# RMSNorm over 16384 rows of 512 on one core: few large transfers, and a first store that waits for a 256-byte marker transfer

## The chip, the cores and the metric

The kernel runs on one core of a Trainium2 chip. The metric is the device time of one execution in microseconds (us); the time before is 161.68 us, the median of three runs (161.65 to 161.87). The core has a matrix engine (PE), a vector engine (VectorE, DVE in the profile), a scalar engine (ScalarE, ACT), GpSimd (POOL) and SyncE (SP). Here SP does no arithmetic: it issues all DMA transfers, in program order, and waits for semaphores before it issues them. 16 DMA engines move the data between device memory (DRAM) and the on-chip memory SBUF.

## What is computed

```python
def reference(x, gamma):                # x: 16 x 1024 x 512 float32, gamma: 512 (ones)
    eps = 1e-5
    rms = np.sqrt(np.mean(x ** 2, axis=-1, keepdims=True) + eps)
    return (x / rms * gamma).astype(np.float32)
```

Each of the 16384 rows of 512 numbers is divided by the root of its mean square and multiplied by gamma. x has 33.55 MB, and the output as much again.

## The kernel before

**Tiles.** The rows are cut into four tiles t = 0 to 3. In a tile each of the 128 partitions holds R = 32 consecutive rows, 64 KB in one piece in DRAM and in SBUF. A whole tile is 8.39 MB. SBUF has three slots of that size; tile 3 goes into slot 0 again, so its loads wait until the stores of tile 0 from the same rows have landed. Everything is done in place: x is loaded into a slot, scaled there, and stored from there.

**Transfers.** `load(t, slot, r0, r1)` (line 45) and `store(t, slot, r0, r1)` (line 49) move rows r0 to r1 of all 128 partitions. One such transfer is 128 descriptors, one for each partition, 2 KB times the number of rows each, eight on each of the 16 DMA engines. All go through SP's one queue. gamma is brought as a single row, in five pieces (line 58), each a single descriptor on one DMA engine. The list before loads row 0, rows 1 to 7, gamma, rows 8 to 15 and rows 16 to 31 of tile 0, then the first half of tile 1. Then, in `transfers`, come stores of one single row of tile 0 between the next loads. The rest of tile 0 is stored in two pieces, tile 3 is loaded in two halves, and tiles 1 and 2 are stored whole and tile 3 in halves.

**Groups.** The arithmetic goes by groups of rows, `(t, first row, rows, pieces, share)`: `pieces` says how many rows the ScalarE and VectorE instructions for the sums of squares take at a time, `share` how many rows at the end of the group GpSimd scales. For one group:

- `square_sums`: ScalarE squares a piece into a scratch tile (line 96), VectorE adds it up along the row (line 97). A piece of 7 or 4 rows goes to PSUM (the memory that the matrix engine writes), a piece of 5 to its own SBUF tile, and a piece of 9 rows into rows 23 to 31 of slot 2, which is free as long as tile 2 has not been loaded there.
- `inverse_rms`: ScalarE takes the root (line 102), VectorE the reciprocal (line 103).
- `scale_by_pool`: GpSimd multiplies its share of the rows by the reciprocal (line 109) and by gamma (line 110).
- `scale` and `times_gamma`: ScalarE multiplies the other rows one by one by the reciprocal (line 118), then VectorE multiplies them all by gamma (line 122), which a matmul of ones with the gamma row has spread over the partitions in PSUM (line 66).

The order is written by hand (`manual_schedule`). While group k is scaled, the squares of group k+1 are taken; `transfers(t, g)` of group k is called after its `times_gamma`, so its DMAs follow all earlier DMAs in SP's order. The engines run their own instructions in that order and wait for each other by semaphores. DMA transfers use eight semaphores in turn, so the ninth transfer waits until the first has landed.

Of the kernel before, what the change touches and what calls it, by code (L numbers as in the profile page):

```python
# [9 lines left out]
def kernel(  # L10
# [6 lines left out]
    nc = tc.nc  # L17
    P = nc.NUM_PARTITIONS
    eps = 1e-5
    fp32 = mybir.dt.float32  # L20
# [4 lines left out]
    of = out.flatten_outer_dims()  # L25
    N, D = xf.shape
# [9 lines left out]
    const = ctx.enter_context(tc.tile_pool(name="const", bufs=1))  # L36
# [7 lines left out]
    def load(t, slot, r0, r1):  # L44
        dma = nc.sync.dma_start(out=slots[slot][:, r0:r1], in_=xv[t][:, r0:r1])  # L45
        before_scale.append((slot, r0, r1, dma))

    def store(t, slot, r0, r1):
        dma = nc.sync.dma_start(out=ov[t][:, r0:r1], in_=slots[slot][:, r0:r1])
        before_scale.append((slot, r0, r1, dma))  # L50

    gamma_row = const.tile([1, D], fp32)
    pieces = (0, 128, 224, 320, 416, D)

    load(0, 0, 0, 1)
    load(0, 0, 1, 8)
    for c0, c1 in zip(pieces, pieces[1:]):
        nc.sync.dma_start(out=gamma_row[:, c0:c1], in_=gamma.unsqueeze(0)[:, c0:c1])
    load(0, 0, 8, 16)
    load(0, 0, 16, 32)  # L60
    load(1, 1, 0, 16)

    ones_col = const.tile([1, P], fp32)
    nc.gpsimd.memset(ones_col, 1.0)  # L64
# [9 lines left out]


    groups = [
        (0, 0, 7, (7,), 3),
        (0, 7, 9, (9,), 5),
        (0, 16, 16, (7, 9), 7),
        (1, 0, 16, (7, 9), 7),  # L80
        (1, 16, 16, (7, 5, 4), 7),
        (2, 0, 16, (7, 5, 4), 7),
        (2, 16, 16, (7, 5, 4), 7),
# [36 lines left out]
    def times_gamma(t, g, r0, r1):  # L120
# [4 lines left out]
        for slot, b0, b1, earlier in before_scale:  # L125
            if slot == slot_of[t] and b0 < g + r1 and g + r0 < b1:
                tc.declare_no_dep(scaled.ins, earlier.ins, reason="ScalarE waited for it before it scaled these rows")

    def transfers(t, g):
        if (t, g) == (0, 0):  # L130
            store(0, 0, 0, 1)
            load(1, 1, 16, 32)
            store(0, 0, 1, 2)
            load(2, 2, 0, 23)
        elif (t, g) == (0, 16):
            store(0, 0, 2, 3)
            load(2, 2, 23, 32)
            store(0, 0, 3, 16)
            store(0, 0, 16, 32)
            load(3, 0, 0, 16)  # L140
            load(3, 0, 16, 32)
        elif (t, g) == (1, 16):
            store(1, 1, 0, 32)
        elif (t, g) == (2, 16):
            store(2, 2, 0, 32)
        elif (t, g) == (3, 0):
            store(3, 0, 0, 16)
        elif (t, g) == (3, 16):
            store(3, 0, 16, 32)
# [16 lines left out]
    for k, group in enumerate(groups):  # L166
        t, g, n, pieces, share = group
        mine = n - share
        half = (mine + 1) // 2
        ahead = groups[k + 1 :][:1]  # L170
        ss, todo = pieces_of(ahead[0]) if ahead else (None, [])
        scale_by_pool(rstd, t, g, n, share)
        for piece in todo[:2]:
            square_sums(*piece)
        scale(rstd, t, g, 0, half)
        for piece in todo[2:]:
            square_sums(*piece)
        scale(rstd, t, g, half, mine)
        times_gamma(t, g, 0, mine)
        transfers(t, g)  # L180
        for nxt in ahead:
            rstd = inverse_rms(ss, nxt[2])
# [30 lines left out]
```

## Time and profile before

| what | value |
|---|---|
| runs | 161.65, 161.68, 161.87 us |
| profiled execution, first to last instruction (span; its only time on the page) | 160.2 us |
| VectorE busy | 112.0 us, 70% |
| ScalarE busy | 107.8 us, 67% |
| GpSimd busy | 106.4 us, 66% |
| PE busy | 2.0 us |
| HBM read and written | 33.56 MB and 33.55 MB |
| first DMA issue, last DMA issue (SP) | 0.74 us, 139.2 us |

The profiled execution is a separate execution; the page gives its span, from the first to the last instruction. The runs measure the whole execution, which includes what lies before and after. The DMA rows of the page say how busy the 16 DMA engines were on average. The trace also keeps each DMA packet (a descriptor's start, duration and bytes) and each increment of a transfer's semaphore, sixteen for a transfer over all engines; "landed" here means that the last of the sixteen has come. Times are in us from the start of the span.

### The profile page before, as it was taken

What the parts mean: (1) busy time and instruction counts of PE and PEld (TensorE: products, weight loads), DVE (VectorE), ACT (ScalarE), POOL (GpSimd) and SP (SyncE); (2) the same over time, 40 slices, a digit from 0 to 9 for tenths busy, and PEclk for the clock granted to TensorE, in tenths of its full rate; (3) what the DMA queues carried; (4) which work ended last, traced back from release to release, by engine and by line L of the source; (5) the groups of instructions that cost most, each with busy time, mean ns of one, the idle gap of its engine ahead of it and who ended that gap; (6) DMA issues with size and microseconds to landing.
All of it is one profiled execution on the core that took longest, in us unless ns stands there. A gap on an engine that the chain in (4) does not pass through costs nothing.

```text
span 160.2 us, 276 instructions
## 1 busy us (share of the span) xinstructions
PE 2.0 (1%) x2; PEld 0.5 (0%) x2; DVE 112.0 (70%) x39; ACT 107.8 (67%) x108; POOL 106.4 (66%) x24
## 2 busy tenths in 40 slices
PE   0050000000000000000000000000000000000000
PEld 0010000000000000000000000000000000000000
DVE  0018098899798999999999999999999009700000
ACT  3071967976999998999899899989960990000000
POOL 1000951994999599999999999999999980000000
DMA  5999999899999899999999999996996996999994
GB/s 189 431 421 475 442 401 458 340 446 491 417 435 494 388 379 383 426 450 475 434 401 426 483 401 393 524 491 295 524 491 295 524 491 295 401 491 417 401 450 196
DMA packets 2747, 67.12 MB, mean 419 GB/s; under 512 B 313, under 2 KB 314, under 8 KB 826
## 3 DMA queue, kind: packets, MB, share of 16 engines
q1 hardware_dynamic: 2746, 67.11, 98.1%
q14 instruction: 1, 0.01, 0.0%
HBM read 33.56 MB, written 33.55 MB: 419 GB/s over the span
## 4 chain that ended last, share of the span: by engine, by line
DVE 59%; ACT 22%; DMA 4%; ACTq 0%; issue 0%; SPq 0%
DVE ss L97 36%; DVE slot L122 23%; ACT slot L118 8%; ACT slot L96 7%; ACT sq_psum L96 6%; DMA slot<-in_x_dram 4%; DVE ss L103 1%; ACT ss L102 1%; ACTq L208 0%; ACT gamma_b L165 0%; SPq L45 0%; ACTq L96 0%
## 5 line engine op out<-in xcount | busy, mean ns | idle before, releaser
L109 POOL TENSOR_TENSOR slot<-slot,ss 128x3584 f32<-128x3584 f32 (+2 forms) x9 | 47.0, 5218 | 24.1 <-DVE ss L103 24.1
L110 POOL TENSOR_TENSOR slot<-slot,gamma_b 128x3584 f32<-128x3584 f32 (+2 forms) x9 | 59.3, 6587 | 0.7
L97 DVE TENSOR_REDUCE ss<-sq_psum 128x7 f32<-128x3584 f32 (+1 forms) x13 | 42.2, 3247 | 13.7 <-ACT sq_psum L96 13.7
L118 ACT ACTIVATE slot<-slot,ss 128x512 f32<-128x512 f32 x75 | 47.3, 706 | 4.7 <-DVE ss L103 4.7
L122 DVE TENSOR_TENSOR slot<-slot,gamma_psum 128x4608 f32<-128x4608 f32 (+2 forms) x9 | 41.3, 4590 | 8.7 <-ACT slot L118 8.7
L96 ACT ACTIVATE sq_psum<-slot 128x3584 f32<-128x3584 f32 (+1 forms) x13 | 34.6, 2658 | 6.4 <-DMA slot<-in_x_dram 5.7
L97 DVE TENSOR_REDUCE ss<-slot 128x9 f32<-128x4608 f32 x3 | 14.9, 4954 | 4.4 <-ACT slot L96 4.2
L97 DVE TENSOR_REDUCE ss<-sq_sbuf 128x5 f32<-128x2560 f32 x5 | 14.0, 2803 | 0.0
L96 ACT ACTIVATE slot<-slot 128x4608 f32<-128x4608 f32 x3 | 12.1, 4033 | 0.0
L96 ACT ACTIVATE sq_sbuf<-slot 128x2560 f32<-128x2560 f32 x5 | 11.6, 2321 | 0.0
L102 ACT ACTIVATE ss<-ss,eps_t 128x16 f32<-128x16 f32 (+2 forms) x9 | 2.7, 305 | 11.9 <-DVE ss L97 11.9
L103 DVE RECIPROCAL ss<-ss 128x16 f32<-128x16 f32 (+2 forms) x9 | 2.1, 236 | 0.4 <-ACT ss L102 0.4
L66 PE MATMUL gamma_psum<-gamma_row,ones_col 1*128 1x512 f32 x2 | 2.0, 1122 | 8.6 <-DMA gamma_row<-in_gamma_dram 8.6
L72 ACT ACT_TABLE_LOAD x1 | 1.3, 1283 | 1.2 <-PEq L197 1.2
L165 ACT COPY gamma_b<-gamma_psum 128x512 f32<-128x512 f32 x1 | 0.6, 567 | 0.0
L66 PEld LDWEIGHTS gamma_psum<-gamma_row,ones_col 1*128 1x128 f32 x2 | 0.5, 308 | 8.6 <-issue 8.6
L64 POOL MEMSET ones_col<- 1x128 f32 x1 | 0.2, 195 | 0.3 <-POOLq L197 0.3
L197 POOL MEMSET const-float32-0.0<- 128x1 f32 x1 | 0.1, 99 | 0.2 <-issue 0.2
L72 ACT ACTIVATE table<-eps_t 128x1 f32<-128x1 f32 x1 | 0.2, 202 | 0.0
L197 POOL MEMSET const-bfloat16-1.0<- 128x1 bf16 x1 | 0.1, 102 | 0.0
L197 POOL MEMSET const-uint8-127<- 128x1 uint8 x1 | 0.1, 102 | 0.0
L197 POOL MEMSET const-float32-1.0<- 128x1 f32 x1 | 0.1, 99 | 0.0
(1 smaller groups left out, 0.1 us busy)
## 6 DMA issues: line engine op xcount, KB each, us to landing
slot<-in_x_dram SPq DMA_DIRECT2D x5, 4096.0 KB, 21.9
out_dram<-slot SPq DMA_DIRECT2D x3, 4096.0 KB, 23.4
slot<-in_x_dram SPq DMA_DIRECT2D x1, 5888.0 KB
out_dram<-slot SPq DMA_DIRECT2D x1, 3328.0 KB, 21.8
slot<-in_x_dram SPq DMA_DIRECT2D x1, 2304.0 KB, 14.3
slot<-in_x_dram SPq DMA_DIRECT2D x1, 2048.0 KB, 9.9
slot<-in_x_dram SPq DMA_DIRECT2D x1, 1792.0 KB, 7.0
out_dram<-slot SPq DMA_DIRECT2D x3, 256.0 KB
```

The lines of the kernel that those rows point to most:

```text
L66: nc.tensor.matmul(gamma_psum[:, 0], ones_col, gamma_row, start=True, stop=True)
L72: nc.scalar.activation(out=table, in_=eps_t, func=AF.Sqrt)
L96: nc.scalar.activation(out=sq[:, :m], in_=rows, func=AF.Square)
L97: nc.vector.tensor_reduce(out=ss[:, r : r + m, 0], in_=sq[:, :m], axis=mybir.AxisListType.X, op=OP.add)
L102: nc.scalar.activation(out=ss[:, :n, 0], in_=ss[:, :n, 0], func=AF.Sqrt, bias=eps_t, scale=1.0 / D)
L103: nc.vector.reciprocal(out=ss[:, :n, 0], in_=ss[:, :n, 0])
L109: nc.gpsimd.tensor_tensor(out=part, in0=part, in1=by_row, op=OP.mult)
L110: last = nc.gpsimd.tensor_tensor(out=part, in0=part, in1=gamma_b.to_broadcast([P, share, D]), op=OP.mult)
L118: nc.scalar.activation(out=x[:, g + r, :], in_=x[:, g + r, :], func=AF.Copy, scale=rstd[:, r])
L122: scaled = nc.vector.tensor_tensor(out=part, in0=part, in1=gamma_psum.to_broadcast([P, r1 - r0, D]), op=OP.mult)
L165: nc.scalar.copy(out=gamma_b[:, 0], in_=gamma_psum[:, 0])
L197: nc = _bacc.Bacc("TRN2", target_bir_lowering=False, num_devices=1)
```

## The change

The transfers are fewer and larger, one wait is added twice, and two groups become one.

- Tile 0's first half is one load of 16 rows (before: rows 0, 1 to 7, 8 to 15), gamma one piece of 2 KB (before: five). All of tile 1 is loaded ahead of the first group; before, its second half came behind a one-row store.
- The three one-row stores of tile 0 are gone. Tile 2 is loaded as 28 and 4 rows (before 23 and 9), tile 0 stored as 27 and 5 rows (before 1, 1, 1, 13 and 16), tile 3 loaded as 27 and 5 rows (before 16 and 16).
- Between the two loads of tile 2 stands a load of 64 numbers of gamma (256 bytes) into a small tile `mark` that nothing reads. The store of tile 0's rows 0 to 26 waits for it.
- The store of tile 1 waits for the load of tile 3's first 27 rows.
- The first two groups (7 rows and 9 rows, GpSimd shares 3 and 5) become one of 16 rows with a share of 7. The group of tile 1's first half takes its squares in pieces of 7, 5, 4 instead of 7, 9.

```diff
@@ load, store, first loads
-    def store(t, slot, r0, r1):
+    def store(t, slot, r0, r1, behind=None):
         dma = nc.sync.dma_start(out=ov[t][:, r0:r1], in_=slots[slot][:, r0:r1])
         before_scale.append((slot, r0, r1, dma))
+        if behind is not None:
+            tc.add_manual_dep(
+                dma.ins,
+                behind.ins.name,
+                mybir.DependencyInfo(mybir.DependencyClass.Sync, mybir.DependencyReason.DATA),
...
+            )
-    pieces = (0, 128, 224, 320, 416, D)
-    load(0, 0, 0, 1)
-    load(0, 0, 1, 8)
+    pieces = (0, D)
+    load(0, 0, 0, 16)
     for c0, c1 in zip(pieces, pieces[1:]):
         nc.sync.dma_start(out=gamma_row[:, c0:c1], in_=gamma.unsqueeze(0)[:, c0:c1])
-    load(0, 0, 8, 16)
     load(0, 0, 16, 32)
     load(1, 1, 0, 16)
+    load(1, 1, 16, 32)
@@ groups
-        (0, 0, 7, (7,), 3),
-        (0, 7, 9, (9,), 5),
+        (0, 0, 16, (7, 9), 7),
         (0, 16, 16, (7, 9), 7),
-        (1, 0, 16, (7, 9), 7),
+        (1, 0, 16, (7, 5, 4), 7),
@@ transfers
+    last_load = {}
+    mark = const.tile([1, 64], fp32)
+
     def transfers(t, g):
         if (t, g) == (0, 0):
-            store(0, 0, 0, 1)
-            load(1, 1, 16, 32)
-            store(0, 0, 1, 2)
-            load(2, 2, 0, 23)
+            load(2, 2, 0, 28)
+            last_load[2] = nc.sync.dma_start(out=mark, in_=gamma.unsqueeze(0)[:, :64])
+            load(2, 2, 28, 32)
         elif (t, g) == (0, 16):
-            store(0, 0, 2, 3)
-            load(2, 2, 23, 32)
-            store(0, 0, 3, 16)
-            store(0, 0, 16, 32)
-            load(3, 0, 0, 16)
-            load(3, 0, 16, 32)
+            store(0, 0, 0, 27, behind=last_load[2])
+            store(0, 0, 27, 32)
+            last_load[3] = load(3, 0, 0, 27)
+            load(3, 0, 27, 32)
         elif (t, g) == (1, 16):
-            store(1, 1, 0, 32)
+            store(1, 1, 0, 32, behind=last_load[3])
```

More of the change, by code (lines that the diff above doesn't have):

```diff
@@ L46, in load @@
         before_scale.append((slot, r0, r1, dma))
-    def store(t, slot, r0, r1):
+        return dma
+    def store(t, slot, r0, r1, behind=None):
         dma = nc.sync.dma_start(out=ov[t][:, r0:r1], in_=slots[slot][:, r0:r1])
         before_scale.append((slot, r0, r1, dma))
+        if behind is not None:
[3 more added lines that the diff above has]
+                mybir.DependencyInfo(mybir.DependencyClass.Sync, mybir.DependencyReason.DATA),
+                reason="the queue gets this store when the load ahead of it is nearly through",
+            )
     gamma_row = const.tile([1, D], fp32)
-    pieces = (0, 128, 224, 320, 416, D)
-    load(0, 0, 0, 1)
-    load(0, 0, 1, 8)
+    pieces = (0, D)
+    load(0, 0, 0, 16)
     for c0, c1 in zip(pieces, pieces[1:]):
         nc.sync.dma_start(out=gamma_row[:, c0:c1], in_=gamma.unsqueeze(0)[:, c0:c1])
-    load(0, 0, 8, 16)
     load(0, 0, 16, 32)
     load(1, 1, 0, 16)
+    load(1, 1, 16, 32)
     ones_col = const.tile([1, P], fp32)
```

## The prediction, made before the changed kernel was run

> **What bounds the kernel now.** I read the page's DMA rows first, then the busy time by stretch, SP's own waits, and the timeline.
>
> ```profile
> span 160.2 us, 276 instructions
> ...
> DMA  5999999899999899999999999996996996999994
> q1 hardware_dynamic: 2746, 67.11, 98.1%
> ```
>
> The DMA engines are busy for 98.1% of the span, while VectorE, the busiest of the others, is at 70%. The 6s late in the row are not idle time: a packet is booked whole where it starts, and a 64 KB packet takes 2.4 us. In the packet records themselves all 16 engines work without a gap from their first packet (1.75 us on the earliest, 2.52 on the latest) to their last (158.1 to 158.98). The stretches show the tail:
>
> ```profile
> core 0: us, PE busy (x) PEld busy (x) DVE busy (x) ACT busy (x) POOL busy (x), PEclk, DMA share, GB/s
> ...
> 140.00:144.00 4.00, 0.00 (x0) 0.00 (x0) 0.00 (x0) 0.00 (x0) 0.00 (x0) 1.00 1.04 451
> ...
> 152.00:156.00 4.00, 0.00 (x0) 0.00 (x0) 0.00 (x0) 0.00 (x0) 0.00 (x0) 1.00 1.04 451
> 156.00:160.20 4.20, 0.00 (x0) 0.00 (x0) 0.00 (x0) 0.00 (x0) 0.00 (x0) 1.00 0.45 195
> ```
>
> All arithmetic is over at 139.14 us; for the last 20 us only stores run. So the chain of waits, which gives VectorE 59%, misleads: it ends with an instruction that finished 20 us before the span. What counts is how many us of work the DMA queue holds, and whether it ever runs dry.
>
> The start-to-start intervals of packets on one engine fix the price of work: 2048 bytes 80 ns, 14336 bytes 532, 32768 bytes 1209.5, 47104 bytes 1736.5, 65536 bytes 2414, loads and stores alike. A line fits all five: 5 ns a descriptor plus 36.76 ns a KB (1000 bytes). A transfer's end mark on an engine costs 6 ns.
>
> **The change part by part.**
>
> *Fewer descriptors.* The bytes stay: 4.194 MB an engine, 154.18 us, before and after. Before there are 19 large transfers, after 14, each 8 descriptors and an end mark on every engine: 5 x (8 x 5 + 6) = 0.23 us gone. The end of one-row transfers takes 0.07 us more: the three one-row stores took 0.656, 0.656 and 0.696 us on the latest engine instead of 8 x 80 + 6 = 0.646. The page "DMA: Bandwidth & Descriptors" of the Trainium skill, section Anatomy of one DMA, fits about 2.0 us of fixed cost to each DMA (issued from GpSimd there); by that, five fewer would bring an estimated 10 us. The 46 ns measured here decide, since the next transfer is always queued.
>
> *Pauses.* Subtracting line prices from the end marks on the latest engine leaves three extra times in loads: 0.29 us (around 30 us), 0.37 (62), 0.23 (100), together 0.89. Each is in the last few descriptors of a load with a store behind it; but two other loads with one-row stores behind them have none. If they come with such handovers, 3 of 5 had one, a mean of 0.18; the changed kernel has two handovers, 0.36, a gain of 0.53. If they come with time spent loading, they stay: 0. At worst both new handovers pay 0.37 and one more comes elsewhere: a loss of 0.22. I take 0.2, between the two explanations. The first 8 rows cost 0.46 us above their price on the latest engine; the 32 KB descriptors that now go first are not in this trace: between 0 and twice that, and I take the same.
>
> *Start of the arithmetic.* ScalarE's first squares began at 8.31 us, when 8 rows were in. Now they wait for 16 rows. Before, the same bytes had landed at 13.12 us, so about 13.0. From there with the durations of the timeline:
>
> ```profile
> 28.45 4.03 ACT L96 ACTIVATE slot<-slot 128x4608 f32<-128x4608 f32 x1
> 28.55 3.89 DVE L97 TENSOR_REDUCE ss<-sq_psum 128x7 f32<-128x3584 f32 x1 [1.10 <-ACT sq_psum L96]
> ...
> 32.51 4.95 DVE L97 TENSOR_REDUCE ss<-slot 128x9 f32<-128x4608 f32 x1
> ...
> 39.90 6.16 POOL L109 TENSOR_TENSOR slot<-slot,ss 128x3584 f32<-128x3584 f32 x1 [2.23 <-DVE ss L103]
> ...
> 46.14 7.81 POOL L110 TENSOR_TENSOR slot<-slot,gamma_b 128x3584 f32<-128x3584 f32 x1
> ...
> 49.83 0.33 SPq L45 DMA_DIRECT2D slot<-in_x_dram  x1
> ...
> 72.09 10.27 SPq L45 DMA_DIRECT2D slot<-in_x_dram  x2
> ```
>
> Group 0: squares of 7 and 9 rows to 20.1, the second sum to 25.1, root and reciprocal to 25.7. Group 1: squares 25.8 to 32.9, second sum 32.9 to 37.9; nine scalings to 38.4; times gamma 38.5 to 43.4; reciprocal 43.6; GpSimd 43.7 + 6.16 + 7.8 = 57.65. From then on a group takes 13.69 us, as in the timeline (VectorE's products start at 64.07, 77.75, 91.44). This puts VectorE 1.8 us behind the old schedule; it was not the bound. gamma now arrives at about 12.5 us instead of 8.5, and its first reader needs it at 25.3.
>
> *The queue, engine 0* (first packet 1.75, 0.46 extra, line prices, no pauses): four loads of 9.68 us and gamma end at 41.0; tile 2's 28 rows at 57.9, its 4 rows 2.45 us later at 60.4; store of 27 rows to 76.7, of 5 to 79.8; load of 27 to 96.1, of 5 to 99.1; store of tile 1 to 118.4, tile 2 to 137.8, tile 3's halves to 147.5 and 157.1. Now each wait in SP's order:
>
> - Load of tile 2, 28 rows: rows 23 to 27 are scratch until 37.9. Issue to first packet was 1.01 us (0.74 to 1.75), and 1.78 on the latest engine: 39.7 at the latest, against 41.0. Queued behind it are the marker and the 4 rows, issued within 1 us.
> - Store of tile 0: the marker follows 28 rows on one engine. gamma's first piece landed 0.53 us after the load ahead of it ended (7.205 to 7.74), so 58.45; rows 0 to 26 are ready at 57.65. Cover: the 2.45 us of the 4 rows, less 0.53 and 0.02 for SP: 1.9 us for an issue that took 1.01 to 1.78.
> - Load of tile 3, and store of tile 1: each waits for all engines. Cover 3.06 us (5 rows), less the spread of the engines 0.65 to 0.88 and landing 0.36 (71.71 to 72.07): 1.8 to 2.05 us.
> - Squares of tile 3 wait for its 27 rows, landed at about 97.5; before, 16 rows landed at 91.46. ScalarE wants them at 93.6. This 4 us stall moves the last groups: tile 2 ready at 115.4 (its store is due at 118.4), tile 3 at 129.6 and 144.6 (due at 137.8 and 147.5). Less 1.01 us of issue, about 1.9 us remain in the tightest cases; beyond that the loss is us for us.
>
> So the added waits are covered, all of them narrowly. **Sum**: 160.17 - 0.23 - 0.07 - 0.2 = 159.7 of span. Around the span lie 161.68 - 160.17 = 1.5 us, unchanged: 161.2 us, 0.3% faster.
>
> **The rivals.**
>
> *The waits cost more than their cover (slower).* The only start from an empty queue in the trace is the first one. If a late issue needs 2.3 us to its first packet, the marker's handover loses 0.4 us, the other two 0.25 to 0.5 each: about 1.1, so 162.3. The point is 1.9 us; up to there nothing is lost. For it: three covers within 0.2 us of the slowest engine's 1.78. Against it: late engines start late and also run dry late, so 1.01 is the fairer number, and then 0.8 to 0.9 us stay.
>
> *Nothing to measure.* The pauses belong to loading, or the first load costs more: only the 0.30 us of descriptors and one-row tails remains, or less: 161.4 to 161.7, 161.5 as a value. For it: the pauses' places vary, and bytes decide 154.2 of 160.2 us.
>
> *The marker does not do what it says.* If it lands early, the store is held by GpSimd's 57.65 us; if late, it is the first rival. Early: the store simply queues behind the 4 rows, which the old kernel did throughout without a gap: 161.2 to 161.4.
>
> **How the numbers follow.** About 0.2%, 0.32 us, is what a measurement of this kernel can tell from no change. Forecast (queue never dry, some pauses gone; 160.6 to 161.4): 0.5, of which 0.46 is faster beyond 0.32. Nothing to measure: 0.25, all of it same but 0.03 slower. Waits too long: 0.18, slower. Early marker: 0.07, nearly all faster. Faster 0.53, same 0.26, slower 0.21. The ends of the unknown costs are 161.68 - 0.3 - 0.89 - 0.46 = 160.0 and 161.68 - 0.3 + 0.22 + 0.46 = 162.1; taking the lowest tenth off below and reaching a good part of the slow rival above: 160.5 to 162.2.
>
> **What would show it.** Right: 14 large transfers; packet gaps of zero from 2 to 158 us; DMA share over 98%; the first store issued near 58.5 and the store of tile 1 near 97.5 while packets of the pieces ahead still run; ScalarE waiting about 4 us for tile 3; last issue near 144.7. Wrong: engines without packets after 60.4, 79.8 or 99.1 (waits too long), or after 41.0, 118.4, 137.8 or 147.5 (arithmetic too late). A time above 162 would mean a gap; below 160.5 that the pauses and the start cost fell together.

## The result, and the profile after

The changed kernel takes **162.33 us** (median of 8 runs, 161.89 to 162.51) against 161.68 for the kernel before in the same session. The ratio is 1.0035, with a 95% interval of 1.0025 to 1.0045: by the medians it is 0.65 us slower. The ratio is taken over the fast runs and is not the quotient of the two medians, which would be 1.0040. The forecast was 0.5 us faster.

The same rows of the changed kernel's page as were shown for the kernel before:

```profile
span 160.6 us, 256 instructions
...
DMA  7999999999999779999979999899799799799992
...
q1 hardware_dynamic: 2020, 67.11, 97.5%
```

There are 2020 packets instead of 2746, for the same bytes. The DMA engines are a little less busy than before, 97.5% of a longer span; over 98% had been named as a sign of being right. The profiled execution took 162.35 us, and its last packet ended at 159.40. In all profiled executions of this study whose time is known the time was 2.9 to 3.5 us more than the end of the last packet, so that end gives the time to within 0.6 us.

SP's part of the timeline shows when each transfer was issued (start, length, engine, what):

```profile
...
1.55 36.58 SPq L45 DMA_DIRECT2D slot<-in_x_dram  x4
38.18 0.29 SPq L141 DMA_DIRECT2D mark<-in_gamma_dram  x1
38.51 0.33 SPq L45 DMA_DIRECT2D slot<-in_x_dram  x1
59.05 0.82 SPq L50 DMA_DIRECT2D out_dram<-slot  x2
77.74 3.95 SPq L45 DMA_DIRECT2D slot<-in_x_dram  x2
98.58 47.07 SPq L50 DMA_DIRECT2D out_dram<-slot  x4
```

These times were forecast well: the first store near 58.5 came at 59.05, the store of tile 1 near 97.5 at 98.58. The last issue was forecast for 144.7 and came at 145.32. The arithmetic also followed the forecast:

```profile
12.85 3.16 ACT L102 ACTIVATE sq_psum<-slot 128x3584 f32<-128x3584 f32 x1 [10.21 <-DMA slot<-in_x_dram]
...
43.54 6.16 POOL L115 TENSOR_TENSOR slot<-slot,ss 128x3584 f32<-128x3584 f32 x1 [3.82 <-DVE ss L109]
...
49.78 7.81 POOL L116 TENSOR_TENSOR slot<-slot,gamma_b 128x3584 f32<-128x3584 f32 x1
...
98.47 3.16 ACT L102 ACTIVATE sq_psum<-slot 128x3584 f32<-128x3584 f32 x1 [4.95 <-DMA slot<-in_x_dram]
```

Forecast were 13.0 us for the first squares, 57.65 for the end of GpSimd's second share (49.78 + 7.81 = 57.59), and a wait of about 4 us for tile 3 (4.95). The chain of waits now runs through the queue in its middle part:

```profile
38.18 20.80 DMA mark<-in_gamma_dram
...
59.05 18.67 DMA out_dram<-slot
...
77.74 20.71 DMA slot<-in_x_dram
...
98.47 0.02 ACT sq_psum L102
```

The third line is the one to look at. Tile 3's load of 27 rows has a price of 16.31 us on an engine and was issued about 2.2 us ahead of its turn (the turn of a transfer is the moment at which the first engine has finished the transfer queued ahead of it), so with its landing some 19 us were due. It took 20.71.

The loss is found in the packet records. These are the end marks of each transfer on the earliest and on the latest of the 16 engines (us; the price is the line price of the prediction):

```
changed kernel            price   earliest        latest      apart
tile 2 loaded (4 rows)            60.530          60.930      0.40
store 27 rows             16.31   76.840          77.237      0.40
store 5 rows               3.06   79.896          80.498      0.60
load 27 rows of tile 3    16.31   96.542          98.091      1.55
load 5 rows                3.06   99.600         101.395      1.80
store tile 1              19.32  118.947         120.713      1.77
last store                       157.665         159.394      1.73
kernel before
tile 2 loaded                     63.184          63.833      0.65
store 13 rows              7.88   71.058          71.708      0.65
store 16 rows              9.68   80.739          81.389      0.65
load 16 rows of tile 3     9.68   90.420          91.070      0.65
load 16 rows               9.68  100.102         100.984      0.88
last store                       158.102         158.984      0.88
```

Up to 77 us the sixteen engines of the changed kernel are closer together than before. Then the queue goes from stores to loads for the first time. A place where the queue goes from loads to stores or back is called a switch below. The latest end marks lose 0.20 us in the 5 rows stored, 1.28 in the 27 rows loaded and 0.24 in the 5 rows loaded: 1.73 us. The earliest lose 0.34. The steps of the latest mark show where the loss is, but it need not be the same engine each time. After that every transfer takes its price again, so the distance stays to the end. Over all engines the mean end of the last store is 158.23 us, against 158.53 in the kernel before; the last end is 159.39 against 158.98.

### The profile page after: what moved, and what is told of

Read it like the earlier page. It is cut to its first block, busy times and chain, and to the rows that moved or that the text cites. A ratio compares the mean times of both kernels' runs of the same rounds, so it can differ in the third digit from the quotient of the medians.

```text
span 160.6 us, 256 instructions
## 1 busy us (share of the span) xinstructions
PE 2.0 (1%) x2; PEld 0.5 (0%) x2; DVE 112.6 (70%) x38; ACT 108.3 (67%) x109; POOL 104.1 (65%) x22
## 3 DMA queue, kind: packets, MB, share of 16 engines
q1 hardware_dynamic: 2020, 67.11, 97.5%
## 4 chain that ended last, share of the span: by engine, by line
DMA 45%; DVE 22%; ACT 20%; issue 2%; ACTq 0%; SPq 0%
DMA slot<-in_x_dram 20%; DMA mark<-in_gamma_dram 13%; DMA out_dram<-slot 12%; DVE ss L103 12%; DVE slot L128 11%; ACT slot L124 8%; ACT sq_psum L102 5%; ACT slot L102 5%; ACT sq_sbuf L102 1%; ACTq L214 0%; ACT gamma_b L171 0%; DVE ss L109 0%; SPq L45 0%; ACT ss L108 0%; SPq L50 0%
## 5 line engine op out<-in xcount | busy, mean ns | idle before, releaser
L115 POOL TENSOR_TENSOR slot<-slot,ss 128x3584 f32<-128x3584 f32 (+1 forms) x8 | 45.9, 5740 | 31.4 <-DVE ss L109 31.4
L103 DVE TENSOR_REDUCE ss<-sq_psum 128x7 f32<-128x3584 f32 (+1 forms) x14 | 44.5, 3178 | 23.3 <-ACT sq_psum L102 23.3
L116 POOL TENSOR_TENSOR slot<-slot,gamma_b 128x3584 f32<-128x3584 f32 (+1 forms) x8 | 58.0, 7249 | 0.6
L128 DVE TENSOR_TENSOR slot<-slot,gamma_psum 128x4608 f32<-128x4608 f32 (+1 forms) x8 | 41.7, 5213 | 8.9 <-ACT slot L124 8.9
L103 DVE TENSOR_REDUCE ss<-sq_sbuf 128x5 f32<-128x2560 f32 x6 | 16.8, 2803 | 0.0
L102 ACT ACTIVATE sq_sbuf<-slot 128x2560 f32<-128x2560 f32 x6 | 13.9, 2321 | 0.0
L103 DVE TENSOR_REDUCE ss<-slot 128x9 f32<-128x4608 f32 x2 | 9.9, 4953 | 0.1
L102 ACT ACTIVATE slot<-slot 128x4608 f32<-128x4608 f32 x2 | 8.1, 4028 | 0.0
L108 ACT ACTIVATE ss<-ss,eps_t 128x16 f32<-128x16 f32 x8 | 2.4, 304 | 7.8 <-DVE ss L103 7.8
L109 DVE RECIPROCAL ss<-ss 128x16 f32<-128x16 f32 x8 | 2.0, 245 | 0.4 <-ACT ss L108 0.4
L73 PE MATMUL gamma_psum<-gamma_row,ones_col 1*128 1x512 f32 x2 | 2.0, 1122 | 12.9 <-DMA gamma_row<-in_gamma_dram 12.9
L73 PEld LDWEIGHTS gamma_psum<-gamma_row,ones_col 1*128 1x128 f32 x2 | 0.5, 306 | 12.9 <-issue 12.9
```

Source lines behind the costliest of these rows:

```text
L73: nc.tensor.matmul(gamma_psum[:, 0], ones_col, gamma_row, start=True, stop=True)
L102: nc.scalar.activation(out=sq[:, :m], in_=rows, func=AF.Square)
L103: nc.vector.tensor_reduce(out=ss[:, r : r + m, 0], in_=sq[:, :m], axis=mybir.AxisListType.X, op=OP.add)
L108: nc.scalar.activation(out=ss[:, :n, 0], in_=ss[:, :n, 0], func=AF.Sqrt, bias=eps_t, scale=1.0 / D)
L109: nc.vector.reciprocal(out=ss[:, :n, 0], in_=ss[:, :n, 0])
L115: nc.gpsimd.tensor_tensor(out=part, in0=part, in1=by_row, op=OP.mult)
```

## What lengthens: the packets at the switch

Some first packets of the load of 27 rows (55296 bytes; price 2041 ns as a duration):

```
start us   duration ns   longer by
79.903        2605          564
79.902        3033          992
80.199        2082           41
80.270        2044            3
80.303        3394         1353
80.622        3069         1028
80.975        2856          815
```

They do not start late: engines stood without a packet for 0.08 us on average. They take longer, and unevenly. In the kernel before, all 16 packets at the same switch (near 81 us) took their price. For the runs below, "added time" is what packets took beyond their line price as a duration (8 ns + 36.76 ns a KB), summed over the packets of more than 1000 bytes that are over by more than 25 ns and divided by 16, so that it is a mean per engine. It comes from the one profiled execution of each kernel, while the verdict on the time comes from all runs.

## The experiments

Ratios are to the kernel before in the same session; its median was between 161.48 and 161.64 us there. The runs with e were made on chip 13, those with g on chip 10, h on 12 and k on 0, so that a kernel of one letter and a kernel of another differ in the chip too.

### Is it the cover of the first load of tile 3?

**e1_cover8** and **e2_cover3** change one size, the rows that stand in the queue while the load is issued.

```diff
-            store(0, 0, 0, 27, behind=last_load[2])
-            store(0, 0, 27, 32)
-            last_load[3] = load(3, 0, 0, 27)
-            load(3, 0, 27, 32)
+            store(0, 0, 0, 24, behind=last_load[2])    # e2: 29 for 24
+            store(0, 0, 24, 32)
+            last_load[3] = load(3, 0, 0, 24)
+            load(3, 0, 24, 32)
```

> The changed kernel with tile 0 stored and tile 3 loaded as 24 and 8 rows instead of 27 and 5, so that 8 rows of stores (4.9 us) instead of 5 (3.06 us) stand in the queue while the first load of tile 3 is issued. Theory A (a load that is issued behind stores needs up to about 3.4 us until all engines run it at full speed, and had only 2.2): no lengthened first packets at that place, the 16 engines stay within 0.5 us of each other to the end, time about 160.8 (160.5 to 161.2). Theory B (a switch from stores to loads costs this on some engines, whatever the cover): spread and time as in the changed kernel, 162.1 to 162.5. Theory C (the marker and the later first store cost the time): also 162.1 to 162.5.

> The changed kernel with 29 and 3 rows instead of 27 and 5: 1.84 us of stores behind the first piece. Theory A: each us of cover less costs about one us on the late engines, 163.3 to 163.8, and gaps without packets appear near 79 us. Theory B and C: 162.1 to 162.6. The store of tile 1 then has 1.84 us of cover too; if its issue needs more than about 1.0 us, a second gap near 100 us adds up to 0.5 us.

Measured: e1 163.09 us, ratio 1.0087 (1.0062 to 1.0113); e2 162.04 us, 1.0026 (1.0003 to 1.0049). More cover was slower and less cover not slower, the opposite of theory A. In e1's profile SP issued the load at 75.95 us, 4.0 us ahead of its turn (79.98):

```profile
...
58.89 0.82 SPq L50 DMA_DIRECT2D out_dram<-slot  x2
75.95 5.50 SPq L45 DMA_DIRECT2D slot<-in_x_dram  x2
96.76 47.08 SPq L50 DMA_DIRECT2D out_dram<-slot  x4
```

The added time near 80 us was 0.44 us all the same, and there was a second place: the store of tile 1, issued at 96.76, 3.1 us ahead of its turn, had 0.66 us of added time in the loads just ahead of it. Engines ended 2.17 us apart. In e2 the load was issued 1.1 us ahead of its turn, added time near 80 us was 0.83 us, but even: the engines ended 0.49 us apart, and the mean end was 0.49 us later than in the changed kernel. So a late issue of this load is not what it takes, and these two profiles suggest that the time goes by how unevenly the added time falls: e2's last packet ended at 158.98 us, e1's at 160.15.

### Is it the marker?

**e3_no_mark** takes the marker and its wait out.

```diff
-            last_load[2] = nc.sync.dma_start(out=mark, in_=gamma.unsqueeze(0)[:, :64])
-            store(0, 0, 0, 27, behind=last_load[2])
+            store(0, 0, 0, 27)
```

> The changed kernel without the 256-byte marker and its wait: the first store is issued when the arithmetic is ready, near 57.7 us instead of 59.05. Theory A and B: no difference to the changed kernel, 162.1 to 162.6, since no packet was late at the first store. Theory C: most of the loss is gone, 161.2 to 161.6.

Measured: 162.63 us, 1.0064 (1.0036 to 1.0092). Theory C falls: nothing came back. The store was issued at 57.65 us, 3.3 us ahead of its turn, and now the loads ahead of it had 0.60 us of added time (58 to 61 us), where the changed kernel had none; near 80 us stood 0.48 as before. The marker does spare its own switch.

### Are the pauses of the kernel before at fixed places?

**e4_before_again** is the kernel before, profiled once more.

> The kernel before, profiled once more. If the pauses of 0.29, 0.37 and 0.23 us in its loads belong to its order of transfers, they stand at the same places again; if they come by chance, at others or not at all, and the span moves by what they sum to.

Measured: 161.44 us (one run). Around 30 us there was added time again (0.47 us; 0.27 in the first profile). At 62 us it was 0.03 instead of 0.38, at 100 us 0.01 instead of 0.22; 0.05 stood near 40 us, where the first profile had none. So only the pause ahead of the first one-row store came back; by this one repeat the other two are chance. At the switch near 81 us there was none in either profile. The last engine ended at 158.49.

### Issue early or late, small pieces or large ones

**e5** makes the load of tile 3 early and the store of tile 1 late:

```diff
-            store(0, 0, 0, 27, behind=last_load[2])
-            store(0, 0, 27, 32)
-            last_load[3] = load(3, 0, 0, 27)
-            load(3, 0, 27, 32)
+            store(0, 0, 0, 16, behind=last_load[2])
+            store(0, 0, 16, 32)
+            load(3, 0, 0, 16)
+            load(3, 0, 16, 28)
+            last_load[3] = nc.sync.dma_start(out=mark2, in_=gamma.unsqueeze(0)[:, :64])
+            load(3, 0, 28, 32)
```

> The changed kernel with tile 0 stored as 16 and 16 rows, so that tile 3's first load is issued about 9 us ahead of its turn, and with tile 3 loaded as 16, 12 and 4 rows and a second 256-byte marker ahead of the 4 rows, for which the store of tile 1 waits: that store is issued 1 to 2 us ahead of its turn. Theory D (what costs is a load that is issued less than some 5 us ahead of its turn behind stores, and a store that is issued more than some 2 us ahead of its turn behind loads: packets on both sides of the switch grow longer, unevenly over the engines): no lengthened packets after the first 3 us, engines within 0.4 us of each other, 160.8 to 161.2, better than the kernel before. Theory E (the small descriptors of 6 to 16 KB ahead of the switch from stores to loads cost it): the same here, since the pieces are large at that switch. Theory F (each switch costs by chance, whatever the issue): 161.8 to 162.5.

Measured: 162.55 us, 1.0074 (1.0045 to 1.0102). Theory D falls for the load. In SP's part of e5's timeline

```profile
...
58.89 0.85 SPq L50 DMA_DIRECT2D out_dram<-slot  x2
71.20 10.39 SPq L45 DMA_DIRECT2D slot<-in_x_dram  x2
...
98.36 42.94 SPq L50 DMA_DIRECT2D out_dram<-slot  x4
```

the load is issued at 71.20, 9.0 us ahead of its turn (8.7 in the kernel before), and its neighbours have the kernel before's sizes. Yet 0.48 us were added near 80 us, most of it in the last store packets, and the engines ended 1.20 us apart. For the store D held: issued 1.25 us ahead of its turn, it added nothing near 100 us.

**e6** splits the second store in front of the early load into 11 and 5 rows; **e7** also makes the load wait for a marker between these two:

```diff
-            store(0, 0, 16, 32)
-            load(3, 0, 0, 16)
+            store(0, 0, 16, 27)
+            third = nc.sync.dma_start(out=mark, in_=gamma.unsqueeze(0)[:, :64])    # e7 alone
+            store(0, 0, 27, 32)
+            load(3, 0, 0, 16, behind=third)    # e6: without behind
```

> As e5, with tile 0's second half stored as 11 and 5 rows, so that 10 KB descriptors stand ahead of the switch to loads, while the first load of tile 3 is still issued about 9 us ahead of its turn. Theory D: as e5, 160.8 to 161.2. Theory E: as the changed kernel, about 162.2, with lengthened packets near 80 us. Theory F: 161.8 to 162.5.

> As e6, with one more 256-byte marker between the stores of 11 and 5 rows, for which the first load of tile 3 waits: that load is issued about 2 to 2.5 us ahead of its turn, as in the changed kernel, and has 16 rows. Theory D: lengthened packets near 80 us again, 0.3 to 0.6 us on the mean engine and over 1 us on some, 161.8 to 162.4. Theory E: the same as e6. If the 27-row descriptors of the first load were the cause, no lengthening here.

Measured: e6 163.03 us, 1.0095 (1.0062 to 1.0128), 0.41 us added near 80; e7 163.00 us, 1.0064 (1.0032 to 1.0096), 0.62 us. With e5 at 0.48, neither the size of the pieces nor the time of issue tells these apart; theory E falls with D. Theory F (chance at each switch) is not settled by this; e5 and e6 lie above its range of 161.8 to 162.5. In e6 a single engine ended 1.36 us behind the fifteenth.

**e8** drops the second marker's wait:

```diff
-            store(1, 1, 0, 32, behind=last_load[3])
+            store(1, 1, 0, 32)
```

> As e5 without the wait of tile 1's store for the second marker: it is issued near 86 us, 14 us ahead of its turn. Theory D: load packets shortly before 100 us grow longer by 0.2 to 0.6 us a engine, 161.2 to 161.6, about what the kernel before has. Theories E and F: no difference to e5.

Measured: 163.47 us, 1.0118 (1.0105 to 1.0132), slower than any of the theories had it. The store, issued at 85.78, added 0.91 us to the loads of 4 rows ahead of it (97 to 100 us), on top of 0.53 near 80. Theory F had forecast no difference to e5, so it does not hold for this switch.

### From the kernel before: which part brings it?

**g1** puts the new end on the old kernel, **g2** takes the one-row stores out of it, **g3** puts one-row stores into the changed kernel, **g4** puts the new start of the queue on the old kernel.

```diff
# g1, in the kernel before
-            store(0, 0, 3, 16)
-            store(0, 0, 16, 32)
-            load(3, 0, 0, 16)
-            load(3, 0, 16, 32)
+            store(0, 0, 3, 27)
+            store(0, 0, 27, 32)
+            last_load[3] = load(3, 0, 0, 27)
+            load(3, 0, 27, 32)
-            store(1, 1, 0, 32)
+            store(1, 1, 0, 32, behind=last_load[3])
# g2, in the kernel before
-            store(0, 0, 0, 1)
-            store(0, 0, 1, 2)
-            store(0, 0, 2, 3)
-            store(0, 0, 3, 16)
+            store(0, 0, 0, 16)
# g3, in the changed kernel, between the marker and load(2, 2, 28, 32)
+            store(0, 0, 0, 1)
+            store(0, 0, 1, 2)
+            store(0, 0, 2, 3)
-            store(0, 0, 0, 27, behind=last_load[2])
+            store(0, 0, 3, 27, behind=last_load[2])
# g4, in the kernel before
-    pieces = (0, 128, 224, 320, 416, D)
-    load(0, 0, 0, 1)
-    load(0, 0, 1, 8)
+    pieces = (0, D)
+    load(0, 0, 0, 16)
-    load(0, 0, 8, 16)
+    load(1, 1, 16, 32)    # behind load(1, 1, 0, 16), and no longer behind the first one-row store
```

> The kernel before, with the changed kernel's pieces from the first long store on: tile 0 stored as rows 3 to 26 and 27 to 31, tile 3 loaded as 27 and 5 rows, tile 1's store behind the 27 rows. Everything ahead of that, with the three one-row stores, is as before. Theory G (the one-row stores between the loads are what spares the kernel before the lengthened packets at the switch near 80 us): no lengthening there, 161.3 to 161.7. Theory H (the pieces and issue times at the end do it): lengthened packets near 80 us, 161.9 to 162.5. Theory I (the start does it: the large first load, the arithmetic 2 us later): 161.3 to 161.7.

> The kernel before without the three one-row stores: rows 0 to 2 of tile 0 go with the first long store, which has 16 rows now; loads and their pieces as before. Theory G: lengthened packets near 79 to 81 us as in the changed kernel, 0.4 to 0.6 us on the mean engine, 161.9 to 162.8. Theory H and I: none there, 161.2 to 161.6.

> The changed kernel with three one-row stores of tile 0 between tile 2's loads of 28 and 4 rows, ahead of the first long store, which then has rows 3 to 26. Theory G: no lengthening at the switch near 82 us, 161.0 to 161.6. Theory H and I: lengthened there as in the changed kernel, 162.1 to 162.7.

> The kernel before with the changed kernel's start of the queue: tile 0's first half as one load, gamma in one piece, both halves of tile 1 ahead of the one-row stores; groups and everything from the first one-row store on as before. Theory G and H: as before, 161.2 to 161.6. Theory I: lengthened packets near 80 us, 161.9 to 162.5.

Measured, with the added time at each place:

| kernel | time us | ratio (interval) | ahead of the first store | near 80 us | engines apart at the end |
|---|---|---|---|---|---|
| g1 | 161.71 | 1.0021 (1.0004 to 1.0039) | 0.26 near 30, 0.27 near 62 | 0.10 | 0.66 |
| g2 | 161.99 | 1.0028 (1.0018 to 1.0038) | 0.93, 56 to 61 us | 0 | 0.62 |
| g3 | 163.36 | 1.0112 (1.0088 to 1.0135) | 1.12, 55 to 57 us | 0.42 | 1.38 |
| g4 | 162.03 | 1.0034 (1.0016 to 1.0052) | 0.95, 38 to 41 us | 0 | 0.85 |

G falls: without one-row stores (g2) the switch near 80 us is clean, and with them (g3) it is not. H falls: the new end on the old kernel (g1) has a mere 0.10 us there. I falls: g4's time lies in its range, but g4 is clean near 80 and has its added time at 38 to 41 us. But a pattern appears. g2, g4 and the kernel before issue their first stores early, and pay just ahead of the first store; then the switch near 80 us costs nothing. The changed kernel pays nothing ahead of its first store, and pays near 80. In the kernel before the first one-row store was issued 4.4 us ahead of its turn (31.76), and the first long store 12.9 us ahead (63.18); these are two lines of SP's part of its timeline:

```profile
27.35 0.35 SPq L49 DMA_DIRECT2D out_dram<-slot  x1
...
50.25 5.48 SPq L49 DMA_DIRECT2D out_dram<-slot  x2
```

SP's part of g2's timeline has the first store at 50.22 us, 11 us ahead of its turn (61.5):

```profile
...
50.22 5.48 SPq L49 DMA_DIRECT2D out_dram<-slot  x2
72.15 10.36 SPq L45 DMA_DIRECT2D slot<-in_x_dram  x2
```

### Arithmetic, or the late first store?

**h2** has the old start and the old groups with the new transfers; **h3** is g2 with only the first store made late (and the last 9 rows of tile 2 cut in 5 and 4 for it); **h5** is the changed kernel with nothing made late.

```diff
# h3, against g2
-            load(2, 2, 23, 32)
-            store(0, 0, 0, 16)
+            load(2, 2, 23, 28)
+            last_load[2] = nc.sync.dma_start(out=mark, in_=gamma.unsqueeze(0)[:, :64])
+            load(2, 2, 28, 32)
+            store(0, 0, 0, 16, behind=last_load[2])
# h5, in the changed kernel; store(0, 0, 0, 16) is now called with group (0, 0)
-            last_load[2] = nc.sync.dma_start(out=mark, in_=gamma.unsqueeze(0)[:, :64])
-            store(0, 0, 0, 27, behind=last_load[2])
-            store(0, 0, 27, 32)
-            last_load[3] = load(3, 0, 0, 27)
-            load(3, 0, 27, 32)
-            store(1, 1, 0, 32, behind=last_load[3])
+            store(0, 0, 0, 16)
+            store(0, 0, 16, 32)
+            load(3, 0, 0, 16)
+            load(3, 0, 16, 32)
+            store(1, 1, 0, 32)
# h2, in the kernel before: the changed kernel's transfers, load(2, 2, 0, 28) called with group (0, 7)
-        (1, 0, 16, (7, 9), 7),
+        (1, 0, 16, (7, 5, 4), 7),
```

> The kernel before in its start and its groups (7 and 9 rows first; only tile 1's first half takes its squares as 7, 5, 4), with the changed kernel's transfers from tile 2's load on, marker and waits included. Theory J (the arithmetic's groups cause the lengthened packets near 80 us): none there, and none elsewhere, 160.8 to 161.2. Theory K (a late first store spares the packets at the first switch, and the next switch pays): lengthened near 80 us by 0.4 to 0.7 us on the mean engine, 161.9 to 162.5.

> The kernel before without the one-row stores, tile 2 loaded as 23, 5 and 4 rows with the 256-byte marker ahead of the 4 rows, and the first store (16 rows) behind the marker; the rest as before, so tile 3's load and tile 1's store are issued early. Theory J: no lengthened packets at 60 and 80 us, 161.0 to 161.4. Theory K: none at 60, 0.4 to 0.7 us near 80, perhaps more near 100, 161.8 to 162.8.

> The changed kernel without marker and without added waits: tile 0 stored and tile 3 loaded as 16 and 16 rows, the first store issued near 43.4 us, some 17 us ahead of its turn, and everything behind it as early as the data allow. Theory J: lengthened packets near 80 us as in the changed kernel, 162.2 to 163. Theory K: lengthened packets just ahead of the first store, near 58 us (0.6 to 1 us), none near 80 us, 161.8 to 162.2, as the kernel before without one-row stores had.

| kernel | time us | ratio (interval) | ahead of the first store | near 80 us | near 100 us | engines apart at the end |
|---|---|---|---|---|---|---|
| h2 | 162.28 | 1.0038 (1.0011 to 1.0066) | 0 | 0.37 | 0.02 | 1.49 |
| h3 | 162.29 | 1.0045 (1.0018 to 1.0073) | 0 | 0.33 | 0.68 | 1.19 |
| h5 | 162.00 | 1.0026 (1.0003 to 1.0048) | 0.90, 58 to 61 us | 0 | 0.11 | 0.91 |

All three stand with theory K, none with J, though the 0.37 and 0.33 us near 80 are a little less than K's 0.4 to 0.7. All three ran on one chip. The old groups with the new transfers pay near 80 us (h2). The new groups with early transfers pay ahead of the first store and nothing near 80 (h5). The pair g2 and h3 is the cleanest: the first store moves from 11 us ahead of its turn to 1.5, and the added time moves from 56 to 61 us to the next two switches. It moves, but it does not shrink (0.94 us after the start in g2, 1.02 in h3), and the times do not tell the two apart: their intervals, 1.0018 to 1.0038 and 1.0018 to 1.0073, overlap. Nor do they tell h5 (1.0003 to 1.0048) from the changed kernel (1.0025 to 1.0045). Two smaller differences come with h3's late store, the marker and the cut of the last load. Neither accounts for the added time near 80 us by itself: e3 has no marker and 0.48 us there, and h5 has a last load of 4 rows and none. In h5 SP issued the first store at 43.71 us, 17.7 us ahead of its turn (61.41):

```profile
43.71 14.57 SPq L50 DMA_DIRECT2D out_dram<-slot  x2
```

SP's part of h3's timeline, to be held against that of g2:

```profile
...
59.05 0.82 SPq L50 DMA_DIRECT2D out_dram<-slot  x2
71.40 10.25 SPq L45 DMA_DIRECT2D slot<-in_x_dram  x2
83.50 55.91 SPq L50 DMA_DIRECT2D out_dram<-slot  x4
```

### Can both be had?

If the early payment is made once, by a one-row store near 32 us, sharp switches later might be free. **k1** has the kernel before's three one-row stores, **k2** the first one, and both have a marker ahead of the last 4 rows of tile 2 and of tile 3, with the first long store and the store of tile 1 waiting for them.

```diff
# k1, in the kernel before (k2: also without store(0, 0, 1, 2) and store(0, 0, 2, 3), and 1 for 3 below)
-            load(2, 2, 23, 32)
-            store(0, 0, 3, 16)
+            load(2, 2, 23, 28)
+            last_load[2] = nc.sync.dma_start(out=mark, in_=gamma.unsqueeze(0)[:, :64])
+            load(2, 2, 28, 32)
+            store(0, 0, 3, 16, behind=last_load[2])
-            load(3, 0, 16, 32)
+            load(3, 0, 16, 28)
+            last_load[3] = nc.sync.dma_start(out=mark2, in_=gamma.unsqueeze(0)[:, :64])
+            load(3, 0, 28, 32)
-            store(1, 1, 0, 32)
+            store(1, 1, 0, 32, behind=last_load[3])
```

> The kernel before with its three one-row stores, tile 2's last 9 rows loaded as 5 and 4 with the 256-byte marker between, the first long store behind it, and tile 3's second half as 12 and 4 rows with a second marker, tile 1's store behind that. Theory K1 (the first switch pays once, here at the one-row store near 32 us, and sharp switches after it are free): 0.3 to 0.5 us of lengthening near 30 us, none at 60, 80 and 100, 161.0 to 161.4, better than before. Theory K2 (a late store only moves the cost to the next switch, whatever came before): 0.3 to 0.7 us near 80 us, engines over 1 us apart at the end, 161.8 to 162.5.

> As k1 with the first of the three one-row stores alone. Theory K1: as k1, 161.0 to 161.4. Theory K2: as k1, 161.8 to 162.5; near the kernel before without one-row stores and with the late first store, 162.3.

Measured: k1 162.93 us, 1.0061 (1.0037 to 1.0086); k2 162.03 us, 1.0017 (0.9998 to 1.0036). Neither beats the kernel before. Near 30 us they added 0.17 and 0.12 us, at 60 nothing, but near 80 still 0.21 and 0.19. K1 falls: near 80 us the added time was smaller than in the other kernels with a late long store, but not zero, and one profile each does not show that the early payment made it smaller. In k1 one engine ended 1.09 us behind the fifteenth; in k2's profile all ended within 0.43 us of each other, and that execution (161.79 us) was one of the two fastest of its twelve; K2 had forecast over 1 us. k2 is not told apart from the kernel before by its interval. No kernel of the study was faster than the kernel before.

## Why the prediction was wrong

- **What bounds it: right.** The DMA queue sets the time, the arithmetic ends 14 us before the last store is through.
- **Fewer descriptors and no one-row tails: not contradicted.** Transfers that meet no switch keep their line price (16.31, 19.32 and 9.68 us in the table of end marks). No run isolates the term of 0.3 us itself.
- **The start: right.** The first 16 rows cost about the same; added time in the first 8 us was 0.54 us against 0.48.
- **The times of the arithmetic and of the waits: right within 0.6 us up to the load of tile 3, which came 1 us late.** The marker landed at 58.97 instead of 58.45: the engine that carried it started it at 58.33, where 57.9 was forecast (the sixteen engines were through with the 28 rows between 58.06 and 58.44), and from there to the landing it took 0.64 us instead of 0.53.
- **The covers: right that the queue does not run dry.** Engines stood idle for 0.08 us on average near 80 and 0.02 near 100. But the sign that a time above 162 would mean a gap failed: the time is 162.33, and the engines stood idle no longer than that.
- **The pauses: wrong, and this is the step that failed.** I took a gain of 0.2 us and, at worst, "both new handovers pay 0.37". The first handover indeed paid nothing. The next switch, from stores to loads near 80 us, I priced for its cover only, and so at nothing. It added 0.53 us to the mean engine, and the latest end marks lost 1.73 us there. The kernel before had nothing at that switch, and I had read that as a property of the switch. In the nineteen profiles it goes with how the first long store was issued, as said below.
- **One engine for sixteen: wrong.** I added up "engine 0" and carried a spread of 0.65 to 0.88 us along as fixed. It grew to 1.73. The mean engine ended at 158.23 us, 0.30 earlier than in the first profile of the kernel before and level with the second (158.22); the time is the last engine's.
- **The slower rival: right side, wrong mechanism.** It asked for an issue that needs more than 1.9 us; e1 and e5 gave 4 and 9 us and were not faster. That its 162.3 us meets the measured 162.33 is luck. Nor did I have a case in which a wait spares one switch and harms the next.

What the runs show together is this. The added time near 80 us goes with how far ahead of its turn the first long store (13 rows or more) was issued. In the kernel before (both profiles), g1, g2, g4 and h5 it was issued 7.7 us or more ahead, and 0.10 us at most was added at the switch near 80 us. In the other thirteen profiles it was issued 1.4 to 3.6 us ahead, and 0.19 to 0.83 us was added there. In eleven of these the engines ended 1.2 to 2.2 us apart (in h3 most of that came near 100 us); e2 (0.49) and k2 (0.43) are the exceptions. How early the load itself was issued does not sort them: 8.7 us ahead in the kernel before, 2.2 in g1, 9.0 in e5. Nobody tried a first long store between 3.6 and 7.7 us ahead.

The other side is what an early store costs at its own switch. A store that is issued 3 us or more ahead of its turn behind loads can lengthen the load packets ahead of it by 0.6 to 1.1 us an engine (e1, e3, e8, g2, g3, g4, h3, h5), but need not: ahead of its first long store, issued 13 us early, the kernel before had 0.38 us in one profile and 0.03 in the other. A first long store issued 1.4 to 1.7 us ahead lengthened the packets ahead of it by 0.07 us at most.

So the expected gain went into the spread, as far as the profiles can tell. The changed kernel's mean engine ended 0.30 us earlier than the kernel before's in one profile and level with it in the other (158.23 us against 158.53 and 158.22), its last one 0.4 to 0.9 us later (159.39 against 158.98 and 158.49). But the late store is not shown to be what costs the time: h5, which has the new groups and no late store, is 0.26% slower than the kernel before. Kernels with the early store were 0.21 to 0.34% slower than it (g1, g2, g4, h5), those with the late one 0.17 to 1.18%.

What stays open: what in the engines or the memory lengthens the packets at a switch, and why the lead of one store should matter for the next switch. It is also not a plain exchange of one payment for another: e3 and g3, whose first long store was issued 3.3 and 3.6 us ahead, paid at both switches (g3 ahead of its one-row stores, which were issued 16 us early), and the second profile of the kernel before paid next to nothing at 62 and nothing near 80. The spread also differs from execution to execution: the changed kernel's eight runs lie between 161.89 and 162.51 us. One profile of each kernel cannot say how much of its spread is its own.

## What to carry to other kernels

Where a queue is never empty, price the slowest of the 16 DMA engines, not the mean one: compare the first and the last end mark of each transfer, and find the transfer at which they part. Count the places where a queue goes from loads to stores and back, and do not take a free switch in one order of transfers for a free switch in another. In these profiles a wait that kept a store back until its turn left its own switch clean and came with added time at the next, so such a wait has to be tested on the whole kernel.

## What the runs showed of the hardware that was not expected

- At a switch of direction packets of the changed kernel took up to 1353 ns more than their 2041, though no engine ran out of work for long; with the same neighbours, sizes and lead of issue (e5 and the kernel before) one switch had 0.48 us of added time and the other none.
- A store issued only 0.58 us ahead of its turn (e2, 99.42 against 100.00 us) left the engines idle for 0.13 us on average; 1.02 us ahead (changed kernel, 98.58 against 99.60) left 0.02. That is less than the 1.01 to 1.78 us that the very first transfer needed from issue to first packet.
- The Trainium skill, page "DMA: Bandwidth & Descriptors", section Rules for kernel authors, advises at least 1 MiB for a DMA and to coalesce many small transfers into one large one. Taking three 256 KB stores into one larger store here (g2) made the kernel 0.28% slower (0.18 to 0.38); its profile has 0.93 us of added time ahead of the first store, but that this is the reason is not shown. A one-row store cost 0.65 us for 262144 bytes, 94% of the rate of the large ones (80 ns for 2048 bytes an engine against 1209.5 for 32768).
